# A two-block transformer on one core: the first modulation's order written out by hand

## Chip, cores and metric

One core of one Trainium2 chip. The metric is the device time of one execution in microseconds, as the median of several runs. The profile shows one further execution, with a time of its own.

## What is computed

The reference runs two blocks on 256 tokens of width 1024, in 32-bit floats. The first block has a modulated differential attention with a Fourier branch and a routed mixture of 32 experts; the second has two layers with feed-forward nets and two mixers. Only the head of the first block matters here:

```python
mod_l = (silu(c) @ w_ada + b_ada)          # 6 vectors of 1024: shift and scale first
mod_c = (silu(c_ctx) @ w_ada + b_ada)
hl = rms_norm(x, g) * (1 + sc1) + sh1      # 256 tokens
hc = rms_norm(ctx, g) * (1 + csc1) + csh1  # 256 context tokens
pl = hl @ w_in                             # queries, keys, values, Fourier part
pc_kv = hc @ w_in[:, keys and values]
```

## The kernel before

A product of 32-bit floats is made of three products of a rounded format. Each operand is split into a high part (a rounding cast on ScalarE) and a low part (the difference, on VectorE). `mm3` (line 163) then multiplies high by high, high by low and low by high. Weights come as a stream of pieces of 128 x 2048 floats (1 MB). `load` (line 57) issues them on the queue of SyncE (SP) into six raw buffers; a buffer is loaded again when its piece is split (`finished`, line 89). `ahead(n)` (line 125) splits pieces until n lie ready in `wh` and `wl`, of which there are four each; `take` (line 141) hands one out. `high` and `low` (lines 98 and 108) do the two halves of a split by themselves.

`start` (line 782) loads the small inputs and turns c and c_ctx into silu(c), split into `s4`. `first` (line 855) then runs the modulation in four steps k = 0 to 3, each for 256 of the 1024 columns:

- *products with s* (`ada`): two pieces of w_ada, 16 products of 512 columns, onto four rows;
- *m*: ScalarE copies those rows out of PSUM (line 905); four small products turn them upright, "the turn of m";
- *mt*: four VectorE instructions make shift and scale columns (lines 913 and 915);
- `mod_in` (line 917): for the token tiles of x and of the context (w = 0 and 1), four transposes on TensorE, then *hf* = scale and shift (one half on VectorE, line 930, one on ScalarE, line 928), then the split of hf into *xh* and *xl*;
- *k products* (`kprod`): for the four token tiles (0 and 1 of x, 2 and 3 of the context) six products each with w_in's key columns. They add up over the four steps in four banks of PSUM, so step 3 ends them.

Before step 0, each token tile is squared and summed on ScalarE (line 177), its root is taken (lines 184 to 195), and it is scaled (line 883). Behind the modulation, q, v and Fourier products, the attention, the output product, the routing and the experts follow, then the second block.

The order on each engine is set by a scheduler, from the order of the program and from when it expects operands. Each engine then runs its own queue in that order. Semaphores make it wait for the others. SP's loads use eight semaphores in turn, so a load also waits until the eighth before it has landed.

The loop around the change, line 951 on:

```python
            for k in range(4):
                self.ahead(2)
                for w in (1, 0):
                    if w:
                        mods(k)
                    mod_in(k, w)
                ...
                if k < 3:
                    ada(k + 1)
                ...
                kprod(k, kp[k // 2])
```

Of the kernel before, what the change touches and what calls it, by code (L numbers as in the profile page):

```python
# [10 lines left out]
F32 = mybir.dt.float32  # L11
# [3 lines left out]
AF = mybir.ActivationFunctionType  # L15
# [3 lines left out]
P = 128  # L19
T = 2  # L20
D = 1024
EPS = 1e-6
PIECE = 2048
# [6 lines left out]
class Net:  # L30
# [751 lines left out]
    def start(self, ep):  # L782
        nc, I = self.nc, self.I

        rows = ep.tile([40, P], F32, name="rows")
        for o, src in ((0, I["c"][0]), (8, I["c_ctx"]), (16, I["b_ada"][0, : 2 * D]), (32, I["g_mix_norm"][0])):
            n = src.shape[0] // P
            nc.sync.dma_start(rows[o : o + n], src.rearrange("(j p) -> j p", p=P))
        self.idf = self.cp.tile([P, P], F32, name="idf")
        nc.gpsimd.dma_start(self.idf, I["const_eye"])  # L790
        self.limit = self.first_end
        x, c = I["x"][0], I["ctx"][0]
        for n, dst, src in ((1, lambda: self.h[0], x[:P]), (1, lambda: self.h[1], x[P:]),
                            (4, lambda: self.cx[:, 0, :], c[:P]), (4, lambda: self.cx[:, 1, :], c[P:])):
            self.extra.setdefault(n, []).append((dst, src))
        self.lam_in = self.cp.tile([64, 4], F32, name="lam_in")
        self.rope = ep.tile([P, T, 2, 64], F32, name="rope")
        small = [(self.rope, I["const_rope"].rearrange("(t p) i d -> p t i d", p=P))]
        for i, n in enumerate(("lambda_q1", "lambda_k1", "lambda_q2", "lambda_k2")):
            small.append((self.lam_in[:, i : i + 1], I[n].rearrange("o d -> d o")))  # L800
        self.tab = ep.tile([32, 8], F32, name="tab")
        self.hot = ep.tile([32, 256], F32, name="hot")
        for dst, src in small:
            self.extra.setdefault(9, []).append((lambda dst=dst: dst, src))
        for dst, src in ((self.tab, I["rel_table_2"]), (self.hot, I["const_bucket"])):
            self.extra.setdefault(10, []).append((lambda dst=dst: dst, src))
        self.run_loads()
        ps = self.bank()
        nc.tensor.transpose(ps[:, :40], rows, self.idf[:40, :40])
        self.sT = self.cp.tile([P, 8, 2], F32, name="sT")  # L810
        nc.scalar.activation(self.sT, ps[:, :16].rearrange("p (m j) -> p j m", m=2), AF.Silu)
        bg = ep.tile([P, 3, 8], F32, name="bg")
        nc.vector.tensor_copy(bg.rearrange("p i j -> p (i j)"), ps[:, 16:40])
        nc.vector.tensor_scalar_add(bg[:, 1], bg[:, 1], 1.0)
        self.ahead(2)
        return bg

    def ada_pieces(self, i, js=range(0, 8, 2)):
# [36 lines left out]
    def first(self):  # L855
# [3 lines left out]
        with ExitStack() as ctx:  # L859
# [17 lines left out]
            tok = [x[0], x[1], cx[:, 0, :], cx[:, 1, :]]  # L877
            xs = {}

            def scale_in(i):  # L880
                rs = self.rstd(tok[i], D, f"rsf{i}")
                xs[i] = ap.tile([P, D], F32, name=f"xs{i}", tag=f"qz{i}") if i < 2 else tok[i]
                nc.vector.tensor_scalar_mul(xs[i], tok[i], rs)


            mt = ap.tile([P, 2, 8, 2], F32, name="mt")
# [3 lines left out]
                self.xl[i] = pool.tile([P, 8, P], F32R, name=f"xl{i}")  # L890
            pa = {}

            def ada(k):
                ps = self.bank()
                for q in range(2):
                    wh, wl = self.take()
                    for j in range(4):
                        jj = 4 * q + j
                        self.mm(ps[:4], s4[:, jj, :], wh[:, j], start=jj == 0, stop=False)
                        self.mm(ps[:4], s4[:, jj, :], wl[:, j], start=False, stop=jj == 7)  # L900
                pa[k] = ps

            def mods(k):
                m4 = ep.tile([4, 512], F32, name="m4", bufs=1)
                nc.scalar.copy(m4, pa[k][:4])
                ps = self.bank()[:, :8].rearrange("p (i j m) -> p i j m", i=2, j=2)
                for i in range(2):
                    for j in range(2):
                        o = 256 * i + P * j
                        self.mm(ps[:, i, j, :], m4[:, o : o + P], r4, start=True, stop=True)  # L910
# [6 lines left out]
            def mod_in(k, w):  # L917
                ps = self.bank().rearrange("p (j i n) -> p j i n", j=2, i=2)
                for j in range(2):
                    for i in range(2):  # L920
                        o = P * (2 * k + j)
                        nc.tensor.transpose(ps[:, j, i, :], xs[2 * w + i][:, o : o + P], self.idf)
                hf = ep.tile([P, 2, 2, P], F32, name="hf", bufs=2)
                for j in range(2):
                    jj = 2 * k + j
# [9 lines left out]
            kps = {}  # L935

            def kprod(k, pc):
                wh, wl = pc
                for i in (2, 3, 0, 1):
                    if k == 0:  # L940
                        kps[i] = self.bank("acc")
                    for j in range(2):
                        jj = 2 * k + j
                        self.mm3(kps[i], self.xh[i][:, jj, :], self.xl[i][:, jj, :], wh[:, jj % 4, :], wl[:, jj % 4, :],
                                 start=jj == 0, stop=jj == 7)
# [301 lines left out]
    def route_consts(self):  # L1247
# [494 lines left out]
```

## Time and profile before

| | |
|---|---|
| median of 3 runs | 1874.41 us (1873.1 to 1874.9) |
| the profiled execution | 1874.24 us, span 1872.5 us from first to last instruction |
| TensorE, products | 1809.4 us busy, 97% of the span |
| VectorE | 1335.0 us, 71% |
| ScalarE | 1149.1 us, 61% |
| GpSimd (POOL) | 40.1 us, 2% |
| read from HBM | 447.91 MB |

In the rows, PE is TensorE's product and PEld its weight load, DVE is VectorE, ACT ScalarE, POOL GpSimd. A q behind the name marks the queue that issues loads. Times count from the span's start. L161 is line 161 of the kernel, where every product is recorded. Tile names stand as out<-in.

### The profile page before, as it was taken

The page shows a single profiled execution, that of the slowest core. Times are in us where ns is not written, and L with a number is a line of the kernel's source. Part 1 is how long each engine was busy: PE and PEld are TensorE (multiplying, and loading weights), DVE is VectorE, ACT ScalarE, POOL GpSimd, SP SyncE. Part 2 cuts the span into 40 slices and gives each one's busy share as a digit, 9 for nine tenths or more (in the row PEclk, how much of TensorE's full clock was granted, in tenths as well). Part 3 has the DMA queues.
Part 4 walks back from the last instruction along what each step waited for, and adds up shares of the span by engine and source line. Part 5 has one row for each costly group of instructions (what it writes and reads, how often), then busy time and mean ns, then how long its engine had stood idle before and what let it go on. Part 6 is the DMA issues. An engine that isn't in the chain of part 4 may idle for free.

```text
span 1872.5 us, 22794 instructions
## 1 busy us (share of the span) xinstructions
PE 1809.4 (97%) x8305; PEld 1443.0 (77%) x8305; DVE 1335.0 (71%) x2114; ACT 1149.1 (61%) x1912; POOL 40.1 (2%) x73
## 2 busy tenths in 40 slices
PE   5999799999999999899999999999999999999998
PEld 2776567777777776688888888887888888887886
DVE  6987699989899988745567765556555776675554
ACT  5555488888788887644575654456454665465443
POOL 1000000000000000000000000000000011000000
PEclk8999799999999999999999999999999999999999
DMA  9884299999999999556464356654655555665540
GB/s 324 280 278 161 78 359 390 375 391 381 372 379 394 389 389 388 192 182 202 161 222 163 118 197 202 202 180 158 202 193 190 173 177 181 222 217 194 174 169 23
DMA packets 189267, 450.50 MB, mean 241 GB/s; under 512 B 9904, under 2 KB 118840, under 8 KB 164576
## 3 DMA queue, kind: packets, MB, share of 16 engines
q1 hardware_dynamic: 185056, 437.25, 65.3%
q0 software_dynamic: 3808, 11.25, 2.1%
q8 instruction: 66, 1.08, 0.2%
q10 hardware_dynamic: 288, 0.52, 0.1%
q14 instruction: 49, 0.40, 0.1%
HBM read 447.91 MB, written 1.07 MB: 240 GB/s over the span
## 4 chain that ended last, share of the span: by engine, by line
PE 83%; ACT 3%; DVE 2%; issue 1%; DMA 1%; ACTq 0%; DVEq 0%; SPq 0%
PE bank_w L161 59%; PE bank_acc L161 20%; PE bank_w L1524 1%; PE bank_w L316 1%; ACT wh L169 1%; DMA raw<-w_gate 1%; PE bank_w L247 0%; ACT xh L250 0%; PE bank_w L719 0%; ACT L192 0%; DVE wl L113 0%; ACT wh L104 0%; ACT L309 0%; PE bank_w L1487 0%; PE bank_w L507 0%
## 5 line engine op out<-in xcount | busy, mean ns | idle before, releaser
L170 DVE TENSOR_TENSOR wl<-raw,wh 128x512 fp32r<-128x512 f32 (+3 forms) x814 | 522.9, 704 | 252.2 <-ACT wh L169 251.5
L169 ACT CAST wh<-raw 128x512 fp32r<-128x512 f32 (+3 forms) x814 | 461.1, 635 | 268.2 <-PE bank_w L161 204.3
L161 PE MATMUL bank_w<-wh,xh 128*128 128x512 f32 (+2 forms) x1056 | 406.4, 385 | 4.1 <-ACT xh L250 3.4
L161 PE MATMUL bank_w<-wh,xl 128*128 128x512 f32 (+2 forms) x1056 | 402.7, 382 | 0.9 <-DVE xl L251 0.9
L161 PE MATMUL bank_w<-wl,xh 128*128 128x512 f32 (+2 forms) x1056 | 402.5, 381 | 0.0
L113 DVE TENSOR_TENSOR wl<-raw,wh 128x2048 fp32r<-128x2048 f32 x124 | 280.5, 2283 | 0.0
L104 ACT CAST wh<-raw 128x2048 fp32r<-128x2048 f32 x124 | 235.9, 1904 | 7.2 <-DMA raw<-w_gate 5.0
L161 PEld LDWEIGHTS bank_w<-wh,xh 128*128 128x128 f32 x1056 | 199.2, 189 | 42.5 <-ACT xh L250 6.5
L161 PEld LDWEIGHTS bank_w<-wh,xl 128*128 128x128 f32 x1056 | 199.1, 189 | 37.5 <-DVE xl L251 2.2
L161 PEld LDWEIGHTS bank_w<-wl,xh 128*128 128x128 f32 x1056 | 199.1, 189 | 35.0 <-issue 0.2
L161 PE MATMUL bank_w<-wh,XG 128*128 128x512 f32 x388 | 169.8, 438 | 0.0
L161 PE MATMUL bank_w<-wl,XG 128*128 128x512 f32 x388 | 152.2, 392 | 0.0
L161 PE MATMUL bank_acc<-wh,th 128*128 128x512 f32 x352 | 144.2, 410 | 0.0
L161 PE MATMUL bank_acc<-wh,tl 128*128 128x512 f32 x352 | 138.0, 392 | 0.0
L161 PE MATMUL bank_acc<-wl,th 128*128 128x512 f32 x352 | 137.7, 391 | 0.0
L309 ACT ACTIVATE silu<-bank_w,rs 128x256 f32<-128x256 f32 x88 | 41.6, 474 | 153.9 <-PE bank_w L161 153.7
L311 DVE SCALAR_TENSOR_TENSOR hid<-bank_w,rs,silu 128x256 f32<-128x256 f32 x88 | 42.5, 484 | 117.5 <-ACT silu L309 114.3
L161 PE MATMUL bank_w<-raw,act 128*128 128x512 f32 x256 | 115.0, 592 | 0.0
L161 PEld LDWEIGHTS bank_w<-wl,XG 128*128 128x128 f32 x388 | 73.1, 189 | 19.8 <-DVE wlx L113 5.3
L161 PEld LDWEIGHTS bank_w<-wh,XG 128*128 128x128 f32 x388 | 73.0, 188 | 20.0 <-issue 7.4
L161 PEld LDWEIGHTS bank_w<-raw,act 128*128 128x128 f32 x256 | 48.4, 189 | 48.5 <-issue 46.0
L161 PEld LDWEIGHTS bank_acc<-wh,tl 128*128 128x128 f32 x352 | 66.1, 188 | 14.1
(416 smaller groups left out, 2618.3 us busy)
## 6 DMA issues: line engine op xcount, KB each, us to landing
raw<-ffn_w_in SPq DMA_DIRECT2D x176, 512.0 KB, 5.0
raw<-w_gate SPq DMA_DIRECT2D x64, 1024.0 KB, 9.0
raw<-w_up SPq DMA_DIRECT2D x64, 1024.0 KB, 7.5
raw<-w_down SPq DMA_DIRECT2D x64, 1024.0 KB, 7.5
raw<-ffn_w_out SPq DMA_DIRECT2D x44, 1024.0 KB, 5.0
raw<-w_ada SPq DMA_DIRECT2D x16, 1024.0 KB, 5.9
raw<-a_w_in SPq DMA_DIRECT2D x12, 1024.0 KB, 6.5
raw<-b_w_in SPq DMA_DIRECT2D x12, 1024.0 KB, 5.2
```

The source lines that it names most:

```text
L104: self.nc.scalar.copy(wh[:, :k], self.pieces[i][:, :k])
L113: self.nc.vector.tensor_sub(wl[:, :k], raw[:, :k], wh[:, :k].bitcast(F32))
L161: self.nc.tensor.matmul(*a, **k)
L169: self.nc.scalar.copy(h, src)
L170: self.nc.vector.tensor_sub(l, src, h.bitcast(F32))
L309: nc.scalar.activation(s, ps[:, :256], AF.Silu, scale=self.rs[t])
L311: nc.vector.scalar_tensor_tensor(hid[c, t], ps[:, 256:], self.rs[t], s, op0=OP.mult, op1=OP.mult)
L316: nc.tensor.transpose(ps[:, r, :], hid[c, t][:, P * r : P * r + P], self.idf)
L1524: nc.tensor.transpose(tu[which][:, o], gu[which][:, o], self.idf)
```

## The change

All of it is in the head of the first block.

- The stream has one piece of w_in behind step 0's two pieces (before: behind step 1's). The context tokens are loaded right behind it, and no longer behind the first five pieces.
- `start` splits nothing ahead any more. Step 0's two pieces are split in four parts each, the first piece of w_in in two.
- Squares and roots of tokens are separate functions, and so are the parts of `ada`, `mods` and `mod_in`. The tokens of x go through step 0 up to their k products before the context tokens are squared.
- The four steps stand in an order written by hand for TensorE, ScalarE and VectorE (`manual_schedule`). Instructions from outside may still be put in between.
- A root of one column is put at the head of ScalarE's list.
- The two loads of router weights keep their place in GpSimd's order.

```diff
@@ start @@
-        for n, dst, src in ((1, lambda: self.h[0], x[:P]), (1, lambda: self.h[1], x[P:]),
-                            (4, lambda: self.cx[:, 0, :], c[:P]), (4, lambda: self.cx[:, 1, :], c[P:])):
-            self.extra.setdefault(n, []).append((dst, src))
+        for i in range(2):
+            o = slice(P * i, P * i + P)
+            self.extra.setdefault(1, []).append((lambda i=i: self.h[i], x[o]))
+            self.extra.setdefault(2, []).append((lambda i=i: self.cx[:, i, :], c[o]))
...
-        self.ahead(2)
         return bg
@@ first_pieces @@
             self.mod_pieces(k)
-            if k in (1, 2):
-                j = 4 * (k - 1)
+            if k in (0, 2):
+                j = 2 * k
                 self.stream.append((w[:, j : j + 4, 512:1024], (4, 512), True))
@@ first @@
+            def cut():
+                self.high()
+                self.low()
+
+            def cut_parts(n):
...
+                for o in range(0, PIECE, PIECE // n):
+                    o = slice(o, o + PIECE // n)
+                    self.split(wh[:, o], wl[:, o], raw[:, o])
+                    yield
...
-            for i in range(4):
-                scale_in(i)
-            ada(0)
-            kp = []
-            for k in range(4):
-                self.ahead(2)
-                for w in (1, 0):
-                    if w:
-                        mods(k)
-                    mod_in(k, w)
-                if k == 2:
-                    kp.append(self.take())
-                if k < 3:
-                    ada(k + 1)
-                if k == 0:
-                    kp.append(self.take())
-                kprod(k, kp[k // 2])
+            with self.tc.manual_schedule(
+                    engines={mybir.EngineType.PE, mybir.EngineType.Activation, mybir.EngineType.DVE}):
+
+                nc.scalar.activation(ep.tile([P, 1], F32, name="one"), self.idf[:, 0:1], AF.Sqrt)
+                for q in range(2):
+                    list(cut_parts(4))
+                    ada(0, q)
+                square_in(0)
+                square_in(1)
+                mods_out(0)
+                mods_turn(0)
+                scale_in(0)
+                scale_in(1)
+                turn_in(0, 0)
+                mods(0)
+                parts = cut_parts(2)
+                next(parts)
+                mod_in(0, 0)
+                list(parts)
+                kp.append(self.take())
+                kprod(0, 0)
+                kprod(0, 1)
+                square_in(2)
+                square_in(3)
+                scale_in(2)
+                scale_in(3)
+                turn_in(0, 1)
+                self.high()
+                mod_in(0, 1)
+                self.low()
+                self.high()
+                self.low()
+                kprod(0, 2)
+                kprod(0, 3)
+                ada(1, 0)
+                ada(1, 1)
+                self.high()
+                self.low()
+                mods_out(1)
+                for w in range(2):
+                    turn_in(1, w)
+                mods_turn(1)
+                ada(2, 0)
+                mods(1)
+                for w in range(2):
+                    mod_in(1, w)
+                for k in range(1, 4):
+                    first, then = ((0, 1), (2, 3)) if k < 3 else ((2, 3), (0, 1))
+                    ws = (0, 1) if k < 2 else (1, 0)
+                    if k < 3:
+                        cut()
+                    kprod(k, first[0])
+                    if k < 3:
+                        ada(k + 1, 1)
+                        mods_out(k + 1)
+                        if k == 1:
+                            cut()
+                            kp.append(self.take())
+                    kprod(k, first[1])
+                    if k < 3:
+                        for w in ws:
+                            turn_in(k + 1, w)
+                        if k == 1:
+                            cut()
+                    kprod(k, then[0])
+                    if k < 3:
+                        mods_turn(k + 1)
+                    kprod(k, then[1])
+                    if k < 3:
+                        if k == 1:
+                            ada(3, 0)
+                        mods(k + 1)
+                        for w in ws:
+                            mod_in(k + 1, w)
@@ route_consts @@
-        nc.gpsimd.dma_start(self.wr[:, :, :4], I["w_router_group"][0].rearrange("(j p) e -> p j e", j=8))
-        nc.gpsimd.dma_start(self.wr[:, :, 4:], I["w_router_expert"][0].rearrange("(j p) e -> p j e", j=8))
+        for o, n, name in ((0, 4, "w_router_group"), (4, 32, "w_router_expert")):
+            self.tc.keep_in_program_order(
+                nc.gpsimd.dma_start(self.wr[:, :, o : o + n], I[name][0].rearrange("(j p) e -> p j e", j=8)))
```

ScalarE's queue at the middle of the modulation, before: from the last casts of step 0 to those of step 1. The names are tiles with their buffer numbers; a `wh` from a `raw` is the cast of a whole piece, m4 the copy of m.

```order
L169 CAST wh_325<-raw_128 128x2048
L905 COPY m4_331<-bank_w_266 4x512
L169 CAST wh_407<-raw_135 128x2048
L928 ACTIVATE hf_347<-bank_w_342,mt_144 128x256
L928 ACTIVATE hf_359<-bank_w_354,mt_144 128x256
L169 CAST xh2_149<-hf_347 128x256
L169 CAST xh3_151<-hf_347 128x256
L169 CAST xh0_145<-hf_359 128x256
L169 CAST xh1_147<-hf_359 128x256
```

The same place in the changed program, from step 1's hf to step 2's.

```order
L169 CAST xh0_132<-hf_373 128x256
L169 CAST xh1_134<-hf_373 128x256
L961 ACTIVATE hf_380<-bank_w_350,mt_131 128x256
L169 CAST xh2_136<-hf_380 128x256
L169 CAST xh3_138<-hf_380 128x256
L104 CAST wh_387<-raw_154 128x2048
L928 COPY m4_407<-bank_w_360 4x512
L104 CAST wh_409<-raw_176 128x2048
L104 CAST wh_431<-raw_237 128x2048
L961 ACTIVATE hf_467<-bank_w_421,mt_131 128x256
L169 CAST xh0_132<-hf_467 128x256
L169 CAST xh1_134<-hf_467 128x256
```

Before, a step has one whole cast in front of the copy of m and one behind it. In the changed order the two pairs of xh stand apart, then one cast, the copy of m4_407, and two casts behind that copy.

VectorE's queue at the same place, before.

```order
L170 TENSOR_TENSOR wl_326<-raw_128,wh_325 128x2048
L170 TENSOR_TENSOR wl_408<-raw_135,wh_407 128x2048
L913 TENSOR_SCALAR mt_144<-bank_w_333,bg_121 128x2
L915 TENSOR_SCALAR mt_144<-bank_w_333,bg_121 128x2
L913 TENSOR_SCALAR mt_144<-bank_w_333,bg_121 128x2
L915 TENSOR_SCALAR mt_144<-bank_w_333,bg_121 128x2
L930 TENSOR_SCALAR hf_347<-bank_w_342,mt_144 128x256
L930 TENSOR_SCALAR hf_359<-bank_w_354,mt_144 128x256
L170 TENSOR_TENSOR xl2_150<-hf_347,xh2_149 128x256
```

And in the changed program.

```order
L963 TENSOR_SCALAR hf_380<-bank_w_350,mt_131 128x256
L170 TENSOR_TENSOR xl2_137<-hf_380,xh2_136 128x256
L170 TENSOR_TENSOR xl3_139<-hf_380,xh3_138 128x256
L1113 TENSOR_TENSOR lam_in_92<-lam_in_92 64x2
L113 TENSOR_TENSOR wl_388<-raw_154,wh_387 128x2048
L113 TENSOR_TENSOR wl_410<-raw_176,wh_409 128x2048
L113 TENSOR_TENSOR wl_432<-raw_237,wh_431 128x2048
L941 TENSOR_SCALAR mt_131<-bank_w_443,bg_121 128x2
L943 TENSOR_SCALAR mt_131<-bank_w_443,bg_121 128x2
L941 TENSOR_SCALAR mt_131<-bank_w_443,bg_121 128x2
L943 TENSOR_SCALAR mt_131<-bank_w_443,bg_121 128x2
L963 TENSOR_SCALAR hf_467<-bank_w_421,mt_131 128x256
```

Before, two differences of whole pieces (`wl` from `raw`) stand ahead of the four mt; now there are three, and the middle and the last of them belong to the two casts behind the copy of m. Here wl_388 is the half of step 2's weights that the products before m4_407 still need.

Behind step 3's k products the two programs have the same instructions on every engine, with swaps among neighbours for a while, and then in the same order to the end.

## Rows read from the trace of the kernel before

**Rows 1.** Busy time (and count) of each engine by stretch, with granted clock and DMA.

```profile
core 0: us, PE busy (x) PEld busy (x) DVE busy (x) ACT busy (x) POOL busy (x), PEclk, DMA share, GB/s
20.00:30.00 10.00, 0.77 (x7) 0.69 (x7) 9.71 (x19) 8.19 (x10) 0.00 (x0) 0.61 1.06 374
35.00:40.00 5.00, 5.00 (x22) 2.85 (x20) 3.95 (x6) 4.05 (x3) 0.00 (x0) 0.91 1.09 348
75.00:100.00 25.00, 25.00 (x115) 18.95 (x114) 24.05 (x32) 12.29 (x14) 2.34 (x4) 1.00 0.83 283
```

**Rows 2.** SP's waits between 75 and 240 us: total, times, longest.

```profile
SPq L66 <- DVE wl L170: 50.8, 8, 14.7
```

**Rows 3.** Timeline of TensorE (start, us, what): first k product of each step.

```profile
37.66 0.39 PE L161 MATMUL bank_acc<-wh,xh 128*128 128x512 f32 x1
...
48.88 0.40 PE L161 MATMUL bank_acc<-wh,xh 128*128 128x512 f32 x1
...
60.09 0.40 PE L161 MATMUL bank_acc<-wh,xh 128*128 128x512 f32 x1
...
69.41 0.50 PE L161 MATMUL bank_acc<-wh,xh 128*128 128x512 f32 x1 [1.65 <-ACT xh L169]
```

**Rows 4.** Timeline: neighbouring products of 512 columns, early and late.

```profile
12.77 0.63 PE L161 MATMUL bank_w<-wh,s 128*4 128x512 f32 x1
...
13.20 0.63 PE L161 MATMUL bank_w<-wl,s 128*4 128x512 f32 x1
...
37.89 0.39 PE L161 MATMUL bank_acc<-wl,xh 128*128 128x512 f32 x1
```

**Rows 5.** Timeline of TensorE: the turn of m; four transposes.

```profile
43.26 1.05 PE L161 MATMUL bank_w<-r,m 4*128 4x2 f32 x8
...
44.24 0.66 PE L922 MATMUL bank_w<-idf,cx 128*128 128x128 f32 x4
```

**Rows 6.** Groups by shape, 0 to 80 us: count | busy, mean ns | idle before.

```profile
L170 DVE TENSOR_TENSOR wl<-raw,wh 128x2048 fp32r<-128x2048 f32 x14 | 31.9, 2289 | 10.1 <-ACT wh L169 10.0
...
L169 ACT CAST wh<-raw 128x2048 fp32r<-128x2048 f32 x14 | 26.6, 1903 | 13.2 <-DMA raw<-w_ada 7.1 <-PE bank_acc L161 4.8 <-DMA raw<-w_in 0.7
...
L169 ACT CAST xh<-hf 128x256 fp32r<-128x256 f32 x16 | 5.3, 405 | 0.0
...
L928 ACT ACTIVATE hf<-bank_w,mt 128x256 f32<-128x256 f32 x8 | 4.1, 561 | 11.8 <-DVE hf L930 11.8
...
L930 DVE TENSOR_SCALAR hf<-bank_w,mt 128x256 f32<-128x256 f32 x8 | 4.0, 538 | 1.0 <-PE bank_w L922 1.0
...
L905 ACT COPY m<-bank_w 4x512 f32<-4x512 f32 x4 | 2.3, 570 | 0.8 <-PE bank_w L161 0.8
...
L913 DVE TENSOR_SCALAR mt<-bank_w,bg 128x2 f32<-128x2 f32 x8 | 2.2, 275 | 4.4 <-PE bank_w L161 4.4
...
L883 DVE TENSOR_SCALAR xs<-h,rsf 128x1024 f32<-128x1024 f32 x2 | 1.4, 749 | 0.0
```

**Rows 7.** Groups by shape, whole span: quarter pieces on VectorE and ScalarE.

```profile
L170 DVE TENSOR_TENSOR wl<-raw,wh 128x512 fp32r<-128x512 f32 x648 | 403.7, 686 | 202.5 <-ACT wh L169 202.1
...
L169 ACT CAST wh<-raw 128x512 fp32r<-128x512 f32 x648 | 356.1, 621 | 206.3 <-PE bank_w L161 197.0 <-PE bank_acc L161 6.9 <-ACT wh L169 1.8
```

**Rows 8.** Timeline of ScalarE, 8 to 20 us.

```profile
8.11 1.90 ACT L169 CAST wh<-raw 128x2048 fp32r<-128x2048 f32 x1 [3.59 <-DMA raw<-w_ada]
...
13.00 1.90 ACT L169 CAST wh<-raw 128x2048 fp32r<-128x2048 f32 x1 [3.00 <-DMA raw<-w_ada]
...
14.80 1.05 ACT L177 ACTIVATE junk<-h 128x1024 f32<-128x1024 f32 x1
...
17.15 1.28 ACT L192 ACT_TABLE_LOAD   x1
...
18.44 0.29 ACT L192 ACTIVATE rsf<-rsf 128x1 f32<-128x1 f32 x2
...
19.58 1.90 ACT L169 CAST wh<-raw 128x2048 fp32r<-128x2048 f32 x1
```

**Rows 9.** Timeline of GpSimd: the load ahead of which the router's loads stood.

```profile
4.64 0.58 POOL L1073 DMA_DIRECT2D gs<-g_subln  x1
```

More of the change, by code (lines that the diff above doesn't have):

```diff
@@ L878, in first, with square_in @@
             xs = {}
+            def square_in(i):
+                xs[i] = self.sp.tile([P, 4], F32, name=f"rsf{i}", bufs=2)
+                junk = self.sp.tile([P, D], F32, name="junk", bufs=1)
+                nc.scalar.activation(junk, tok[i], AF.Square, accum_out=xs[i][:, 0:1])
             def scale_in(i):
-                rs = self.rstd(tok[i], D, f"rsf{i}")
+                ss = xs[i]
+                self.rsqrt(ss, D)
                 xs[i] = ap.tile([P, D], F32, name=f"xs{i}", tag=f"qz{i}") if i < 2 else tok[i]
-                nc.vector.tensor_scalar_mul(xs[i], tok[i], rs)
+                nc.vector.tensor_scalar_mul(xs[i], tok[i], ss[:, 3:4])
             mt = ap.tile([P, 2, 8, 2], F32, name="mt")
@@ L891, in first, with ada, mods_out, mods_turn @@
             pa = {}
[L893 to L904, printed above, removed]
+            def cut():
+                self.high()
+                self.low()
+            def cut_parts(n):
+                i = self.find(self.cut, True)
+                wh, wl = self.places(i)
+                raw, shape = self.pieces[i], self.stream[i][1]
+                for o in range(0, PIECE, PIECE // n):
+                    o = slice(o, o + PIECE // n)
+                    self.split(wh[:, o], wl[:, o], raw[:, o])
+                    yield
+                self.cutq.append((self.shaped(wh, shape), self.shaped(wl, shape)))
+                self.cut = i + 1
+                self.finished(i)
+                yield
+            def ada(k, q):
+                if q == 0:
+                    pa[k] = self.bank()
+                wh, wl = self.take()
+                for j in range(4):
+                    jj = 4 * q + j
+                    self.mm(pa[k][:4], s4[:, jj, :], wh[:, j], start=jj == 0, stop=False)
+                    self.mm(pa[k][:4], s4[:, jj, :], wl[:, j], start=False, stop=jj == 7)
+            def mods_out(k):
+                m4 = pa[k, 0] = ep.tile([4, 512], F32, name="m4", bufs=1)
                 nc.scalar.copy(m4, pa[k][:4])
-                ps = self.bank()[:, :8].rearrange("p (i j m) -> p i j m", i=2, j=2)
+            def mods_turn(k):
+                ps = pa[k, 1] = self.bank()[:, :8].rearrange("p (i j m) -> p i j m", i=2, j=2)
                 for i in range(2):
@@ L909, in mods @@
                         o = 256 * i + P * j
-                        self.mm(ps[:, i, j, :], m4[:, o : o + P], r4, start=True, stop=True)
+                        self.mm(ps[:, i, j, :], pa[k, 0][:, o : o + P], r4, start=True, stop=True)
+            def mods(k):
+                ps = pa[k, 1]
                 for j in range(2):
@@ L915, in mods, with turn_in @@
                     nc.vector.tensor_scalar_add(mt[:, 0, jj, :], ps[:, 0, j, :], bg[:, 0, jj : jj + 1])
-            def mod_in(k, w):
-                ps = self.bank().rearrange("p (j i n) -> p j i n", j=2, i=2)
+            xt = {}
+            def turn_in(k, w):
+                ps = xt[k, w] = self.bank().rearrange("p (j i n) -> p j i n", j=2, i=2)
                 for j in range(2):
@@ L922, in mod_in @@
                         nc.tensor.transpose(ps[:, j, i, :], xs[2 * w + i][:, o : o + P], self.idf)
+            def mod_in(k, w):
+                ps = xt[k, w]
                 hf = ep.tile([P, 2, 2, P], F32, name="hf", bufs=2)
@@ L933, in mod_in @@
                     self.split(self.xh[2 * w + i][:, o], self.xl[2 * w + i][:, o], hf[:, :, i, :])
[L935 to L939, printed above, removed]
-                    if k == 0:
[L941 to L945, printed above, removed]
@@ L947, in first @@
-            for i in range(4):
-                scale_in(i)
-            ada(0)
-            kp = []
-            for k in range(4):
-                self.ahead(2)
-                for w in (1, 0):
-                    if w:
-                        mods(k)
-                    mod_in(k, w)
-                if k == 2:
-                    kp.append(self.take())
-                if k < 3:
-                    ada(k + 1)
-                if k == 0:
-                    kp.append(self.take())
-                kprod(k, kp[k // 2])
+            kps, kp = {}, []
@@ new lines, in kprod @@
+            def kprod(k, i):
+                wh, wl = kp[k // 2]
+                if k == 0:
+                    kps[i] = self.bank("acc")
+                for j in range(2):
+                    jj = 2 * k + j
+                    self.mm3(kps[i], self.xh[i][:, jj, :], self.xl[i][:, jj, :], wh[:, jj % 4, :], wl[:, jj % 4, :],
+                             start=jj == 0, stop=jj == 7)
+            with self.tc.manual_schedule(
[71 more added lines that the diff above has]
+                            mod_in(k + 1, w)
```

## The prediction

> **What bounds the kernel now.** I read the page's busy shares first (TensorE is far ahead of all others), then the stretches, then the timeline of the first 80 us. A gain or a loss can only sit where TensorE waits. The stretches [rows 1] show the largest such place near the start: between 20 and 30 us it does 0.77 us of work. Behind the modulation there is no slack of that kind: from 75 to 100 us it is busy 25.00 of 25.00 us. From there the program is the same, and the queue of loads waits for VectorE to free buffers [rows 2], not the other way round. So I take a shift of the modulation's end to reach the end of the program in full.
>
> The stage's own beat is in the first k product of each step [rows 3]: 37.66, 48.88, 60.09 and 69.41 us, that is 11.2, 11.2 and 9.3 us a step. Products of 512 columns start 0.43 us apart early in the program (12.77, 13.20) and 0.23 us apart later (37.66, 37.89; [rows 3, 4]): the two levels of the clock, 1.2 and 2.4 GHz. A step is 24 k products (5.5 us), 16 products with s (3.7), 8 transposes (0.13 each) and the turn of m (1.05; both [rows 5]): 11.3 us. The steps are therefore TensorE's own work; its queue hides what ScalarE and VectorE do. That cover is what the change touches.
>
> **What the new order does, priced from rows.** I follow one chain, the first xh tile of each step, since the k products begin with it. Prices of [rows 6]: cast of a whole piece 1.90 us; its difference on VectorE 2.29 (2.24 apart in a row); hf 0.54 on VectorE and then 0.56 on ScalarE (which waits for VectorE's half); xh 0.40 (0.36 apart); m 0.57; four mt 0.8 together; a token's scaling 0.75. Quarter pieces are 0.55 apart on ScalarE and 0.62 on VectorE (busy time over count, [rows 7]). Of halves there is no row; between quarters and wholes they come to about 1.05 and 1.2.
>
> *Up to the first k product.* The second half of step 0's weights is there at 13.00 [rows 8]; four quarter casts end at 15.2. Two squares, 1.18 each (14.80 to 17.15 for two, [rows 8]): 17.6. Then m: 18.1. The table load, 1.28: 19.4. Token 0's root (0.2), three short VectorE steps (0.5) and scaling (0.75): 20.9. Token 1 stands behind all that on VectorE, with a round trip to ScalarE of about 1.05 and another scaling: 22.7. Four mt: 23.5; half a piece: 24.7; hf, hf, xh: **26.3** instead of 37.66, 11.4 us sooner. What was done by then before, and isn't now: the context tokens and step 1's products with s.
>
> *The context half.* On ScalarE stand the second xh, half a cast and two squares (to 30.1); then root, scaling, root, scaling as above (33.3), four transposes (33.9), hf, hf, xh: **35.7**.
>
> *Step 1.* VectorE ends two xl at 36.5 and takes three whole differences; the first two end at 38.8 and 41.0. The last eight products with s end at 43.0; m 43.6; transposes to 43.9; the turn of m 45.0; four mt 45.8; hf, hf, xh: **47.3**. Before, this was 48.88: of the lead 1.6 us are left.
>
> *Steps 2 and 3, where I choose.* The queues shown ahead have, behind step 1's first xh, the rest of both token pairs, then one piece, then the copy of m, then two more pieces, and VectorE's four mt behind all three differences. The copy of m waits for the products with that one piece, so ScalarE can't cast the next two meanwhile. In a row: second pair 2.65, cast 1.90, difference 2.29, eight products 2.0, m 0.57, cast 1.90, differences 2.29 and 2.24, mt 0.8, hf, hf, xh 1.5: 18.1 us, to **65.4**. TensorE has 11.3 us to put beside this and stands for the rest. Step 3: second pair, cast and difference 6.85; then VectorE has eight quarters (5.0) of the query weights and one more whole difference (2.24) in front of mt: 14.1; mt, hf, hf, xh: 16.4, to **81.8**. Before, that product began at 69.41: **+12.4 us**.
>
> *The clock.* At 1.2 GHz each product on the chain costs 0.20 us more. Before, the grant fell during TensorE's pause (0.61 over 20 to 30 us, [rows 1]) and averaged 0.91 again over 35 to 40 us. The new order has pauses of about 5 us ahead of the products with s in steps 2 and 3. I take the fall there: eight products, 1.6 us, twice (in step 3 the last cast waits for a buffer that these products free, so it passes on), and 1.0 us in step 1 after the pause of the context half. That is 4.2 us: 86.0 against 69.4, **+16.6 us**.
>
> *The rest of the edits.* The root of one column takes a table load and an activation ahead of the first weights. ScalarE was idle there for 3.59 us until 8.11 [rows 8], so it costs nothing; without that cover it would be 1.5 us. It spares nothing either: the table of the silu is loaded after it, and the load in front of the token's root is still in the order. The Trainium skill puts a switch of table at a load of 1.28 us and a drain of about 1.4 (ScalarE: Activation LUTs, What ACT_TABLE_LOAD costs); here the root starts at 18.44, right behind the load of 17.15 [rows 8], so the sum has no drain. With one it would be 1.4 us more.
>
> On SP's queue the first piece of w_in and the context, 2.1 MB, go ahead of step 1's pieces: 6.0 us at 348 GB/s [rows 1]. Those pieces were cast from 19.58 on [rows 8], so they come by about 26 and 28 us and are wanted at 32: nothing. On POOL's queue the router's loads go behind the load of g_subln (0.58, [rows 9]) and a short mask, under 1 us. The first casts of step 0's two pieces are 4.9 us apart [rows 8], where 1.05 MB at 348 GB/s takes 3.0; so between nothing and 1.9 us can be won there. I take nothing, the nearer row being that both loads are still issued long before 13.00.
>
> **The sum.** The profiled execution took 1874.24 us (span 1872.5 and 1.7 around it), 0.17 under the median shown. 1874.24 + 16.6 = **1890.8 us**.
>
> **The rivals.**
> 1. *The lead stays (faster).* Place: steps 2 and 3. If ScalarE and VectorE cut their pieces during TensorE's work after all, TensorE's own work sets the end: from 26.3, 72 k products and 48 with s (27.6), 28 transposes (3.6), three turns (3.1): step 3 starts at 60.6, 8.8 us sooner: 1865.4 us. For it: the idle stretch of [rows 1] is real, and seven differences are only 16 us of VectorE. It decides when the two casts behind the copy of m run before that copy. Against it: each engine runs its queue in order, and the order has them behind. 0.06.
> 2. *No change.* The chain overlaps as before, 11.2 and 9.3 us a step from 48.3 (47.3 and the 1.0 of the clock): step 3 starts at 68.8, 1873.6 us. It needs two of the three differences out of mt's way; the order has none. 0.04.
> 3. *The clock stays low* in all steps. The 40 products of a step take 17.2 us at 0.43, with turn and transposes some 20, as long as the chain itself: about 3 us more than my sum, 1893.8 us. For it: the pauses come in each step instead of once. Against it: a step still has 5 us of products in one go. 0.10. The Trainium skill describes a clock that falls again in every round of a kernel that works in bursts between waits (TensorE: Matmul & The Clock Gate, HAM oscillation — how this bites in real kernels); the trace of before shows one such fall at the place of [rows 1].
>
> My forecast has 0.80. A measurement of this kernel tells about 0.2%, 3.7 us, from no change; both +12.4 and +19.6 are beyond it. So slower 0.90, within 0.04, faster 0.06.
>
> **The range.** Below: +12.4 with no fall of the clock, less the 1.9 of the router's loads, 1884.7: I go to 1885. Above: the third rival, 1893.8, and 1 us for the prices of halves and hops: 1895. Left out are the first two rivals, 0.10, and what I have not thought of.
>
> **What would show it.** Right: first k products at about 26, 48, 68 and 86 us; ScalarE's copy of m waiting for TensorE with two casts behind it; TensorE idle for the cast and the difference of one piece in each of steps 2 and 3, with the grant at 0.50 near 55 and 75 us; then the same beat as before, 16 to 17 us later. Wrong: k products less than 12 us apart from step 1 to step 2, or a shift at 75 us that is not there at 230 us.

## The result, and the profile after

The changed kernel takes 1888.53 us in the median of four runs, against 1873.76 of four runs of the kernel before: ratio 1.008, interval 1.0061 to 1.0098. So it is slower by about 0.8%, where 1890.8 was forecast, with 1885 to 1895 as the range. (One of the four runs, at 2065.79 us, is disturbed and left out of the ratio; the others took 1886.8 to 1888.8, with a median of 1888.29.) The profiled execution took 1888.29 us, 14.05 more than that of before.

TensorE's timeline gives the beat: the first k product of each step, and the waits in step 2 (53.44, 55.76) and step 3 (72.83, 75.65). They answer to [rows 3].

```profile
26.55 0.80 PE L161 MATMUL bank_acc<-wh,xh 128*128 128x512 f32 x1 [2.35 <-ACT xh L169]
...
48.98 0.50 PE L161 MATMUL bank_acc<-wh,xh 128*128 128x512 f32 x1 [0.41 <-ACT xh L169]
...
53.44 0.40 PE L161 MATMUL bank_w<-wh,s 128*4 128x512 f32 x1 [2.79 <-ACT wh L104]
55.76 0.59 PE L161 MATMUL bank_w<-wl,s 128*4 128x512 f32 x1 [1.93 <-DVE wl L113]
...
68.38 0.50 PE L161 MATMUL bank_acc<-wh,xh 128*128 128x512 f32 x1 [0.41 <-ACT xh L169]
...
72.83 0.39 PE L161 MATMUL bank_w<-wh,s 128*4 128x512 f32 x1 [2.80 <-ACT wh L104]
75.65 0.59 PE L161 MATMUL bank_w<-wl,s 128*4 128x512 f32 x1 [2.42 <-DVE wl L113]
...
87.08 0.50 PE L161 MATMUL bank_acc<-wh,xh 128*128 128x512 f32 x1 [0.78 <-ACT xh L169]
```

The steps begin at 26.55, 48.98, 68.38 and 87.08 us, where 26.3, 48.3, 68 and 86.0 were forecast. In steps 2 and 3 a single product with s runs when its cast is there, then TensorE stands until the difference is there. The stretches, which answer to [rows 1], tell the same: the hole of before between 20 and 30 us has become smaller, and two new ones stand at 50 and 70 us.

```profile
20.00:30.00 10.00, 4.83 (x12) 3.46 (x13) 7.17 (x21) 5.58 (x11) 0.00 (x0) 0.50 1.09 350
...
40.00:50.00 10.00, 9.59 (x48) 5.18 (x47) 5.58 (x10) 1.85 (x4) 0.00 (x0) 0.97 0.95 302
50.00:60.00 10.00, 5.29 (x15) 2.31 (x14) 3.30 (x5) 4.13 (x6) 0.00 (x0) 0.71 0.35 130
60.00:70.00 10.00, 9.59 (x46) 6.35 (x44) 6.79 (x10) 4.73 (x6) 0.00 (x0) 0.95 0.51 188
70.00:80.00 10.00, 4.78 (x13) 2.24 (x13) 8.65 (x12) 8.50 (x13) 0.00 (x0) 0.73 0.40 132
```

The granted clock fell to the lower level, 1.2 GHz, in both pauses; 0.50 would be that level throughout. The short stretches behind the pauses show it (0.51 and 0.55, and 0.96 between them):

```profile
54.00:60.00 6.00, 4.24 (x11) 2.04 (x12) 1.71 (x1) 1.05 (x2) 0.00 (x0) 0.51 0.45 165
60.00:74.00 14.00, 10.01 (x47) 6.43 (x45) 9.45 (x14) 8.70 (x12) 0.00 (x0) 0.96 0.41 154
74.00:80.00 6.00, 4.35 (x11) 2.16 (x12) 6.00 (x9) 4.53 (x7) 0.00 (x0) 0.55 0.55 173
```

ScalarE's timeline shows what the products waited for. One cast, the copy of m (which waits over 5 us for TensorE), and the next two casts behind that copy:

```profile
51.49 1.89 ACT L104 CAST wh<-raw 128x2048 fp32r<-128x2048 f32 x1
58.95 0.57 ACT L928 COPY m<-bank_w 4x512 f32<-4x512 f32 x1 [5.57 <-PE bank_w L161]
59.43 3.70 ACT L104 CAST wh<-raw 128x2048 fp32r<-128x2048 f32 x2
67.33 0.57 ACT L961 ACTIVATE hf<-bank_w,mt 128x256 f32<-128x256 f32 x1 [4.20 <-DVE hf L963]
67.92 0.71 ACT L169 CAST xh<-hf 128x256 fp32r<-128x256 f32 x2
```

VectorE's timeline: the middle difference at 53.42, then 5.65 us of idle time, then two differences in a row, and only then the four mt.

```profile
53.42 2.29 DVE L113 TENSOR_TENSOR wl<-raw,wh 128x2048 fp32r<-128x2048 f32 x1 [1.28 <-ACT wh L104]
61.36 4.49 DVE L113 TENSOR_TENSOR wl<-raw,wh 128x2048 fp32r<-128x2048 f32 x2 [5.65 <-ACT wh L104]
65.77 0.27 DVE L941 TENSOR_SCALAR mt<-bank_w,bg 128x2 f32<-128x2 f32 x1
```

At the start, ScalarE's timeline answers to [rows 8]:

```profile
9.02 2.18 ACT L169 CAST wh<-raw 128x512 fp32r<-128x512 f32 x4 [3.50 <-DMA raw<-w_ada]
13.50 2.18 ACT L169 CAST wh<-raw 128x512 fp32r<-128x512 f32 x4 [2.31 <-DMA raw<-w_ada]
...
17.82 0.56 ACT L928 COPY m<-bank_w 4x512 f32<-4x512 f32 x1
18.40 1.28 ACT L192 ACT_TABLE_LOAD   x1
19.69 0.20 ACT L192 ACTIVATE rsf<-rsf 128x1 f32<-128x1 f32 x1
```

The quarters, the copy of m and the first product came as worked out. The token's root starts at 19.69, where the table load of 18.40 ends, so no drain shows here either. The first weights came at 9.02 instead of 8.11 though the router's loads were issued later. I come back to that.

### The profile page after: what moved, and what is told of

Its sections match the earlier page's. It is cut to its first block, busy times and chain, and to the rows that moved or that the text cites. A ratio compares the mean times of both kernels' runs of the same rounds, so it can differ in the third digit from the quotient of the medians.

```text
span 1886.5 us, 22810 instructions
## 1 busy us (share of the span) xinstructions
PE 1818.8 (96%) x8305; PEld 1445.5 (77%) x8305; DVE 1338.1 (71%) x2127; ACT 1153.1 (61%) x1927; POOL 40.1 (2%) x73
## 4 chain that ended last, share of the span: by engine, by line
PE 83%; ACT 2%; DVE 1%; issue 0%; ACTq 0%; DVEq 0%
PE bank_w L161 60%; PE bank_acc L161 20%; PE bank_w L1614 1%; PE bank_w L316 1%; ACT wh L169 1%; PE bank_w L247 0%; ACT xh L250 0%; PE bank_w L719 0%; ACT L192 0%; PE bank_w L1577 0%; DVE xl L251 0%; PE bank_w L507 0%; ACT junk L177 0%; DVE wl L170 0%; ACT wh L104 0%
## 5 line engine op out<-in xcount | busy, mean ns | idle before, releaser
L170 DVE TENSOR_TENSOR wl<-raw,wh 128x512 fp32r<-128x512 f32 (+2 forms) x820 | 507.6, 681 | 247.9 <-ACT wh L169 247.5
L169 ACT CAST wh<-raw 128x512 fp32r<-128x512 f32 (+2 forms) x820 | 449.0, 617 | 266.8 <-PE bank_w L161 205.2
L113 DVE TENSOR_TENSOR wl<-raw,wh 128x2048 fp32r<-128x2048 f32 x131 | 296.4, 2285 | 7.0 <-ACT wh L104 6.9
L104 ACT CAST wh<-raw 128x2048 fp32r<-128x2048 f32 x131 | 249.0, 1903 | 4.6 <-DMA raw<-w_gate 2.2
L161 PEld LDWEIGHTS bank_acc<-wh,tl 128*128 128x128 f32 x352 | 66.1, 188 | 14.1
```

Of the source, the lines that this page charges most:

```text
L104: self.nc.scalar.copy(wh[:, :k], self.pieces[i][:, :k])
L113: self.nc.vector.tensor_sub(wl[:, :k], raw[:, :k], wh[:, :k].bitcast(F32))
L161: self.nc.tensor.matmul(*a, **k)
L169: self.nc.scalar.copy(h, src)
L170: self.nc.vector.tensor_sub(l, src, h.bitcast(F32))
```

## The experiments

Times are medians. "Before" ran beside each group of experiments on the same chip, with 1872.0 to 1872.8 us, and the ratios are to those runs; the change itself has its ratio from its own runs above. The last columns are the first k product of each step in each profiled execution.

| kernel | us | ratio to before | step 0 | 1 | 2 | 3 |
|---|---|---|---|---|---|---|
| before | 1872.8 | | 37.66 | 48.88 | 60.09 | 69.41 |
| the change | 1888.53 | 1.0061 to 1.0098 | 26.55 | 48.98 | 68.38 | 87.08 |
| e1, scheduler's order | 1866.05 | 0.9957 to 0.9978 | 24.62 | 44.35 | 53.30 | 63.78 |
| e2, casts ahead | 1878.91 | 1.0026 to 1.0054 | 26.67 | 49.74 | 63.01 | 79.17 |
| e3, before with the loads | 1870.00 | 0.9979 to 0.9997 | 28.36 | 45.13 | 56.36 | 65.73 |
| e4, clock kept up | 1883.74 | 1.0051 to 1.0078 | 26.28 | 46.77 | 64.83 | 81.71 |
| e9, only step 0 by hand | 1873.25 | 1.0003 to 1.0021 | 26.07 | 50.54 | 59.21 | 70.45 |
| e10, only steps 1 to 3 by hand | 1878.47 | 1.0028 to 1.0055 | 25.55 | 41.44 | 60.54 | 78.73 |

The theory is the prediction's: steps 2 and 3 are chained by the place of casts, copy of m and differences. Rival A puts the loss on the clock, rival B on loads that come late.

**e1, the scheduler's order.** The hand-written order is taken away, all else stays:

```diff
-            with self.tc.manual_schedule(
-                    engines={mybir.EngineType.PE, mybir.EngineType.Activation, mybir.EngineType.DVE}):
...
```

> The changed kernel with the hand-written order taken away: the same statements, loads, parts and root, but the scheduler puts the instructions of TensorE, ScalarE and VectorE in order. Theory (the loss sits in the order of casts, copy of m and differences in steps 2 and 3): the loss goes. TensorE's own work is 11.3 us a step, so from a first k product at about 26 the steps stand no further apart than before (11.2, 11.2, 9.3): step 3's first k product lies between 60 (all the lead kept) and 69.4 (as before), the time between 1865 and 1875 us. Rival A (the clock falls in pauses that come from the early first step itself, whoever orders the queues): at least 1883 us. Rival B (w_in's piece and the context tokens ahead of step 1's pieces make these late): slower than 1880 us, with ScalarE's casts of step 1's pieces waiting for a DMA.

It took 1866.05 us, 22.5 less than the change and 6.7 less than before. ScalarE's timeline, and TensorE's busy time in two stretches:

```profile
25.02 3.81 ACT L104 CAST wh<-raw 128x2048 fp32r<-128x2048 f32 x2
...
32.71 3.71 ACT L104 CAST wh<-raw 128x2048 fp32r<-128x2048 f32 x2
38.26 0.57 ACT L928 COPY m<-bank_w 4x512 f32<-4x512 f32 x1 [1.84 <-PE bank_w L161]
38.75 1.90 ACT L104 CAST wh<-raw 128x2048 fp32r<-128x2048 f32 x1
...
43.76 0.58 ACT L928 COPY m<-bank_w 4x512 f32<-4x512 f32 x1 [0.28 <-PE bank_w L161]
```

```profile
40.00:50.00 10.00, 10.00 (x51) 6.66 (x50) 7.89 (x16) 7.12 (x10) 0.00 (x0) 1.00 1.05 361
50.00:60.00 10.00, 10.00 (x48) 6.31 (x46) 8.46 (x17) 6.81 (x15) 1.28 (x2) 1.00 0.98 357
```

The copies of m for steps 1 and 2 stand 5.5 us apart (38.26 and 43.76; in the changed kernel 44.81 and 58.95), because two casts and one cast were done ahead of them. TensorE is busy 10.00 of 10.00 us between 40 and 50 and between 50 and 60. Rivals A and B fall: the early first step and the new loads are all in here. The rest of the change is thus a gain that the written order more than takes back. This run frees the order of three engines at once, so it does not say which engine's order costs what.

**e2, two casts ahead.** The written order, with the piece that step 2's and step 3's last products with s need split one place earlier (`cut` is `high` and `low` in a row):

```diff
-                self.high()
-                self.low()
+                cut()
+                cut()
                 mods_out(1)
...
-                    if k < 3:
-                        cut()
                     kprod(k, first[0])
...
                         mods(k + 1)
+                        if k == 1:
+                            self.high()
                         for w in ws:
                             mod_in(k + 1, w)
+                        if k == 1:
+                            self.low()
```

> The changed kernel, with one cast and one difference moved: the first piece of step 2's second half is cast ahead of step 1's copy of m and its difference taken ahead of step 1's mt; the same piece of step 3 is cast ahead of step 2's hf and its difference taken behind step 2's last xl. Theory: in the changed kernel TensorE waited 2.79 us for that cast and 1.93 for that difference in step 2 (50.65 to 55.76), 2.80 and 2.42 in step 3. In step 2 the copy of m can then come as soon as ScalarE is through the second pair of xh at 51.5 and TensorE through its products, at about 53 instead of 58.95; step 3 loses its cast of 1.9 us and the fall of the clock of 1.4. Step 2's first k product at about 62.5 (68.4 before this edit), step 3's at about 78 (87.1), the time 1879 us, between 1876 and 1882. Rival A (the clock alone): only the falls near 55 and 75 us go, 1.4 us each: 1885 to 1888. Rival B (late loads): 1887 to 1890.

It took 1878.91 us; step 2 began at 63.01 (62.5 expected), step 3 at 79.17 (78). ScalarE's timeline shows the cast at 43.28 ahead of the copy of m, and the next copy at 53.31 instead of 58.95:

```profile
43.28 1.90 ACT L104 CAST wh<-raw 128x2048 fp32r<-128x2048 f32 x1 [3.62 <-PE bank_w L161]
45.37 0.58 ACT L928 COPY m<-bank_w 4x512 f32<-4x512 f32 x1 [0.18 <-PE bank_w L161]
...
53.31 0.57 ACT L928 COPY m<-bank_w 4x512 f32<-4x512 f32 x1 [0.96 <-PE bank_w L161]
53.79 5.51 ACT L104 CAST wh<-raw 128x2048 fp32r<-128x2048 f32 x3
...
71.24 1.90 ACT L169 CAST wh<-raw 128x2048 fp32r<-128x2048 f32 x1 [5.20 <-PE bank_w L161]
73.05 0.57 ACT L928 COPY m<-bank_w 4x512 f32<-4x512 f32 x1
```

So moving one cast and one difference in each of two steps, with TensorE's order as in the change, gives back 9.6 of the 14.8 us (7.9 at step 3's first k product in the profiles). Step 3 keeps 16 us. There the difference for the last products with s is taken only at 66.44, behind all of step 2's xl, and TensorE waits 3.87 us for it. The copy of m (73.05) stands behind one more whole cast, of the weights for the values, for which ScalarE waited 5.20 us until 71.24. VectorE's line and TensorE's:

```profile
66.44 2.29 DVE L113 TENSOR_TENSOR wl<-raw,wh 128x2048 fp32r<-128x2048 f32 x1
```

```profile
68.78 0.40 PE L161 MATMUL bank_w<-wl,s 128*4 128x512 f32 x1 [3.87 <-DVE wl L113]
```

**e3, the loads alone, in the kernel before.**

```diff
...
+            self.extra.setdefault(1, []).append((lambda i=i: self.h[i], x[o]))
+            self.extra.setdefault(2, []).append((lambda i=i: self.cx[:, i, :], c[o]))
...
-            if k in (1, 2):
-                j = 4 * (k - 1)
+            if k in (0, 2):
+                j = 2 * k
...
+                if k == 0:
+                    kp.append(self.take())
                 if k < 3:
                     ada(k + 1)
-                if k == 0:
-                    kp.append(self.take())
```

> The kernel before, with the order of loads of the change and nothing else: the first piece of w_in and the context tokens right behind step 0's pieces (that piece is then also split ahead of step 1's). Theory: no loss from this; step 1's pieces come in time: between 1868 and 1877 us. Rival B: the two pieces of step 1 come 6 us later and all steps move with them: 1878 to 1881 us.

1870.00 us: no loss, and with an interval that ends at 0.9997 a small gain. Rival B falls a second time.

**e4, the clock kept up.** The products of `fill`, whose result nobody reads, stand in TensorE's pauses: 20 in steps 2 and 3 each, and twice 8 in step 0.

```diff
+            def fill(n):
+                ps = self.bank()
+                wh = kp[0][0]
+                for m in range(n):
+                    self.mm(ps[:4], s4[:, 0, :], wh[:, m % 4], start=m == 0, stop=m == n - 1)
...
                     if k < 3:
+                        fill(20)
                         ada(k + 1, 1)
```

> The changed kernel with products that nobody reads put into TensorE's pauses, so that the granted clock stays up: 8 and 8 around the context's transposes in step 0, 20 ahead of the second half of the products with s in steps 2 and 3. The order of ScalarE and VectorE is the change's. Theory (the clock is the smaller part): the products with s behind the pauses take 1.8 us instead of 3.2 in steps 2 and 3, and the context's k products 2.4 us less: 3 to 5 us, so 1883.5 to 1886. Rival A (the clock is the whole loss): near 1874 us. If the added products themselves get into the way, the time rises above 1888.5 and the run tells nothing.

1883.74 us, 4.8 less than the change. From 30 to 90 us its stretches show the clock at 1.00; two of them had 0.71 and 0.73 above:

```profile
50.00:60.00 10.00, 9.74 (x51) 5.70 (x49) 4.49 (x2) 5.37 (x4) 0.00 (x0) 1.00 0.33 117
...
70.00:80.00 10.00, 8.84 (x46) 5.87 (x45) 10.00 (x15) 5.78 (x9) 1.90 (x2) 1.00 0.63 215
```

The added products were through before the difference was there: behind them TensorE still waited 0.26 us for it in step 2 and 1.16 in step 3. So part of the loss is the clock, a third; with the clock up, steps 2 and 3 still begin 18.1 and 16.9 us behind the step before.

**e9 and e10, by place.** The hand-written order for step 0 alone (e9: the `with` block ends behind `kprod(0, 3)`), and for the rest alone (e10: it begins there).

```diff
                 kprod(0, 2)
                 kprod(0, 3)
-                ada(1, 0)
...
+            ada(1, 0)
...
```

> The changed kernel with the hand-written order kept for step 0 alone; from the products with s of step 1 on the scheduler orders the queues. Theory, now split by place: in the scheduler's order (e1) ScalarE casts step 1's pieces from 25.02 on, ahead of the context's half of step 0, and copies step 1's m at 38.26; by hand the first of them is cast at 31.91 and the others from 36.06, behind tokens and context, and m is copied at 44.81. So step 0's order costs 6.5 us against e1 and steps 1 to 3 the other 16: 1872.5 us, between 1869 and 1877. Rival (as the prediction had it: the loss sits in steps 2 and 3, and step 0 by hand is a gain): 1865 to 1868 us.

> The other half: step 0 in the scheduler's order, the products with s of step 1 and all behind them by hand as in the change. Theory split by place: 6.5 us less than the change, 1882 us, between 1879 and 1885. Rival (the loss sits in steps 2 and 3 alone): step 1 comes sooner, but the chains of 18 to 19 us in steps 2 and 3 stay as they are, and the 6.5 us of step 1 are kept too, so also 1882; what tells the two apart is the other run, and here the distance between the first k products of steps 1, 2 and 3: 18 to 20 us each if the chains of steps 2 and 3 don't depend on step 0.

e9 took 1873.25 us, within the range of the theory by place, so step 0's written order costs some 7 us against e1 (7.2 by the medians, 6.7 at step 3's first k product). Its rival, that step 0 by hand is a gain and all of the loss sits in steps 2 and 3, falls. ScalarE's timeline of e9, with the first cast of step 1's pieces at 31.42 (25.02 in e1):

```profile
31.42 1.89 ACT L104 CAST wh<-raw 128x2048 fp32r<-128x2048 f32 x1
...
35.37 3.71 ACT L104 CAST wh<-raw 128x2048 fp32r<-128x2048 f32 x2
...
43.94 0.57 ACT L928 COPY m<-bank_w 4x512 f32<-4x512 f32 x1
```

e10 took 1878.47, less than the 1882 expected and just below the range of 1879 to 1885. Its TensorE timeline:

```profile
41.44 0.50 PE L161 MATMUL bank_acc<-wh,xh 128*128 128x512 f32 x1 [0.42 <-ACT xh L169]
...
60.54 0.50 PE L161 MATMUL bank_acc<-wh,xh 128*128 128x512 f32 x1 [0.41 <-ACT xh L169]
...
78.73 0.50 PE L161 MATMUL bank_acc<-wh,xh 128*128 128x512 f32 x1 [0.79 <-ACT xh L169]
```

The steps stand 19.1 and 18.2 us apart, nearly as in the change (19.4 and 18.7), though step 1 begins 7.5 us sooner: the chain of steps 2 and 3 does not depend on step 0. That places the loss. From e1 to the change, step 1 begins 4.6 us later (48.98 against 44.35) and the way from step 1 to step 3 is 18.7 us longer (38.1 against 19.4). Together 23.3, which is the distance of the two spans (1886.5 and 1863.2).

**The small edits, one at a time, in the scheduler's order.** e5 puts the router's loads behind the Fourier tables' on GpSimd's queue, e6 puts them back where they were before the change, e7 leaves out the root of one column, e8 splits step 0's pieces whole. The diff is e8's.

```diff
-                    list(cut_parts(4))
+                    list(cut_parts(1))
...
-                parts = cut_parts(2)
+                parts = cut_parts(1)
```

> The version in the scheduler's order (e1), with the two loads of router weights behind the loads of the Fourier tables on GpSimd's queue, so that they are issued long behind step 0's pieces and not 1 us later. If these loads take time from step 0's weights, the two first casts of step 0's pieces come sooner than in e1 (there the halves of the first piece land at 6.08 and 8.49, those of the second at 11.15 and 13.00): at best the second piece lands 3.0 us behind the first, 1.5 us sooner, and the time falls by 1 to 2 us against e1's 1866. If they take nothing: the same landings within 0.3 us and the same time.

> The version in the scheduler's order (e1), with the two loads of router weights issued where they were before the change, ahead of g_subln's. The prediction took this edit at nothing, with up to 1.9 us to be won by the later issue. If it is worth something, the time rises by up to 1.9 us here. Against it: in the five profiles with the later issue or with the earlier one, the first piece of step 0 landed at 8.03 and 8.01 with the earlier issue and at 8.49 to 8.94 with the later. By that the edit costs, and the time falls by 0 to 1 us here.

> The version in the scheduler's order (e1), without the root of one column at the head of ScalarE's list. Theory: nothing, since ScalarE waits for the first weights until 8.5 anyway, and the table load in front of the token's root stays in the order: within 1 us of e1. If the root spares a drain or a later load, the time rises by 1.3 us or more.

> The version in the scheduler's order (e1), with step 0's pieces and the first of w_in split whole instead of in four and two parts. A whole cast and difference end 4.2 us behind the landing, four quarters some 2.8: step 0's copy of m comes 1.1 to 1.4 us later, and its first k product with it. If the steps behind carry a lead on, the time rises by 1 to 3 us against e1; if TensorE's own work bounds them, by under 1.

| | us | runs | first casts of step 0's two pieces |
|---|---|---|---|
| e1 | 1866.05 | 1863.6 to 1869.4 | 8.57, 13.08 |
| e5, router late | 1863.37 | 1862.5 to 1867.0 | 8.47, 12.04 |
| e6, router as before | 1865.13 | 1863.3 to 1867.6 | 8.08, 13.70 |
| e7, no root | 1864.24 | 1863.5 to 1865.5 | 9.44, 13.99 |
| e8, whole pieces | 1866.48 | 1865.4 to 1867.3 | 9.04, 13.60 |

The ranges of these kernels overlap with e1's, and no median lies more than 2.7 us from it, so none of these edits is worth more than about 3 us, and most can't be told from nothing. e7 was expected within 1 us of e1 and came out 1.8 below, inside the spread.

e5 alone moves the place it should: step 0's second piece is cast 3.57 us behind the first, where the eight traces with the change's issue of the router's loads have 4.48 to 4.56. Cast at 12.04, it comes 1.0 us sooner than in e1, and the profiled execution ends 2.0 us sooner (1861.2 against 1863.2). By the medians it is the fastest version here, 0.9945 to 0.9973 of before, but it isn't told apart from e1 (0.9957 to 0.9978).

In e8 step 0's product comes 4.3 us later (28.88 against 24.62), where 1.1 to 1.4 were expected. Of that 0.6 us are left at step 1 (44.90 against 44.35), but 2.4 at step 3 (66.19 against 63.78) and at the end of the profile (1865.6 against 1863.2). The medians are 0.4 us apart. So what the parts win in step 0 is at most in part carried on.

The issue of the router's loads a microsecond later, which is what the change does, brings nothing: in the three traces with the earlier issue (before, e3, e6) step 0's pieces are first cast at 8.08 to 8.11 and at 12.27 to 13.70 us, in the eight with the later one at 8.50 to 9.44 and at 13.03 to 13.99. Why the first piece comes later with it, no run here shows: in e5, with these loads out of the way, it is cast at 8.47.

## Why the prediction was right

- *What bounds it.* The pauses of TensorE were the right place to look. The claim that a shift behind the modulation goes through in full holds between e1 and the change: 23.0 us at 270 us, 23.4 at the end. Against the profile of before it holds as far as 230 us, where the shift is 17.8 us (17.7 at step 3), but at the end it is 14.0. The last section says what before lost on the way.
- *Up to the first k product*: 26.3 forecast, 26.55 measured; the context half 35.7 and 35.90. Most prices came from rows; halves, the short VectorE steps and, in steps 2 and 3, the second pair were estimates. By the prices of rows hf, hf and xh take 1.5 us, so the two sums end at 26.2 and 35.4, not at the 26.3 and 35.7 that they state; measured, those three took 1.63 us (24.92 to 26.55, 34.27 to 35.90). And step 0's second piece was cast at 13.50 instead of 13.00. The close fit is thus in part luck.
- *Step 1*: 47.3, and 48.3 with the clock, against 48.98. The lead of 1.6 us was gone. The context's k products ran at the lower clock (granted 0.50 from 34 to 40 us), and the products with s stood behind them. I had 1.0 us for that; e4, where they run at the upper level, starts step 1 2.2 us sooner. This term was too small by half. I also didn't see why step 1 is late at all: e9 shows that the written order of step 0 puts step 1's first cast 6.4 us later than the scheduler's does. I had set the lead of 11.4 us against what step 0 leaves undone, and stopped there.
- *Step 2*: 18.1 us and 1.6 for the clock forecast, 19.4 measured. The chain is the one named: cast (51.49), difference (53.42), products, copy of m (58.95), two casts, two differences (61.36), mt (65.77), hf, xh. e2 shows that it is the cause: with the first cast and its difference ahead it measures 13.3.
- *Step 3*: 16.4 and 1.6 forecast, 18.7 measured. Here a step of the sum was wrong. I had VectorE's quarters and last difference in front of mt as what ends last. They took what I had for them, 14.25 us from step 2's first k product (14.1 forecast), but VectorE was through at 82.6 and then waited 2.13 us for the turn of m. The copy of m (80.21) stood behind one more cast that waited for a buffer, and the turn (83.68) behind eight transposes and six k products. The sum has no such wait, only the 1.6 us of the clock at that place. That the size was off by 0.7 us alone is luck. ScalarE's lines, VectorE's and TensorE's:

```profile
78.41 1.90 ACT L169 CAST wh<-raw 128x2048 fp32r<-128x2048 f32 x1 [1.47 <-PE bank_w L161]
80.21 0.57 ACT L928 COPY m<-bank_w 4x512 f32<-4x512 f32 x1
```

```profile
75.51 7.12 DVE L170 TENSOR_TENSOR wl<-raw,wh 128x512 fp32r<-128x512 f32 x9
84.77 0.28 DVE L941 TENSOR_SCALAR mt<-bank_w,bg 128x2 f32<-128x2 f32 x1 [2.13 <-PE bank_w L161]
```

```profile
83.68 1.05 PE L161 MATMUL bank_w<-r,m 4*128 4x2 f32 x8
```

- *The clock*: 4.2 us in all forecast, 4.8 by e4. The parts fit less well: against e4, steps 2 and 3 lose 1.3 and 1.8 us (1.6 each forecast), and step 1 begins 2.2 us later (1.0). The Trainium skill's picture of a clock that falls again in each round of bursts and waits (TensorE: Matmul & The Clock Gate, HAM oscillation — how this bites in real kernels) agrees with the traces as far as it was used: 0.51 at 54 to 60 us, 0.96 from 60 to 74, 0.55 at 74 to 80. The third rival, a clock that stays low, did not come: between the pauses it rose again, to 0.96 over 60 to 74 us.
- *The rest at nothing*: the root (e7) and the router's loads (e6) are within the spread; the load order even gives a little in the kernel before (e3).
- *The sum*: 1890.8 against 1888.5. At step 3's first k product the shift was 17.7 us, 1.1 more than forecast; the end shows 3.7 less than that place, since the profile of before lost time further on (last section). The two misses have opposite signs, and that they partly cancel is luck.

The first rival, that the lead stays, is what e1 does: step 3 at 63.78 (60.6 in the rival's sum) and 1866.05 us (1865.4). The times agree better than the places, since part of the gain at the end is again what before lost further on. The rival had its condition right, two casts ahead of the copy of m, and the written order has them behind.

## What to carry to other kernels

A written order is judged by the engine that feeds the others: ask for each instruction that waits (here the copy of m) what stands behind it on its queue, and whether the next round needs that. An early start is worth only what the later rounds carry on; here the written order pushed step 1's casts back by 6 us and chained steps 2 and 3, while the same edits in the scheduler's order took 6.7 us less than before. Where a wait must stand in a queue, put the work of the next round ahead of it as far as buffers allow.

## What the runs showed beside that

The profiled execution of before lost some 4 us far behind the change that most other kernels here did not lose, with the same program there: 1.2 us near 510 us (no other trace), about 1.3 near 760 us (only e6 besides), and 1.6 us near 1540 us. The last is the clock. In the stretch around it the changed kernel has 1.00, and e3, which lost as much as before did, 0.93 (first line the change, second e3):

```profile
1535.00:1560.00 25.00, 23.33 (x120) 20.47 (x119) 20.65 (x49) 21.76 (x41) 3.20 (x6) 1.00 0.54 164
```

```profile
1514.00:1539.00 25.00, 23.33 (x112) 20.32 (x111) 20.31 (x47) 20.96 (x40) 3.21 (x6) 0.93 0.54 166
```

Of the twelve traces five (before, e3, e6, e9, e10) have this fall and seven do not; TensorE pauses there twice, 1.18 and 0.49 us, in both. What decides between them, no run here shows. What two single profiles of this kernel say of a microsecond or two must therefore be read at the place of the edit, not at the end.
